# Gates and output projections of two branches with the token tiles stationary instead of the weight tiles

## The chip, the core and the metric

The kernel runs on one core of a Trainium2 chip. The metric is the device time of one execution in microseconds (us); the runs shown before are three executions, and their median is what a change is measured against. A profile is one further execution, with a record of every instruction. Engines are named as in the profile: PE is TensorE, ACT is ScalarE, DVE is VectorE, POOL is GpSimd, SP is the queue that starts most transfers.

## What is computed

One encoder block over 256 tokens of width 2048, in float32, cut here to what matters:

```python
u = rmsnorm(x)
proj = u @ w_in                 # r_q r_k r_v r_g | c_q c_kv k_pe | g_ret g_mla
ry = norm_per_head(retention(rope(r_q), rope(r_k), r_v)) * ret_norm_g
y_ret = (ry * silu(r_g)) @ w_ret_o                  # 8 heads of 256
q, k, v = lora_projections(rmsnorm(c_q), rmsnorm(c_kv), k_pe)
y_mla = attention(q, k, v) @ w_mla_o                # 16 heads of 128
merged = sigmoid(g_ret) * y_ret + sigmoid(g_mla) * y_mla
h = x + merged @ w_out
h = h + square(relu(rmsnorm(h) @ w_up)) @ w_down
return rmsnorm(h)
```

Five products of 256 x 2048 by 2048 x 2048 are touched here: the retention gate `r_g`, the gate `g_ret`, the projection `w_ret_o`, the gate `g_mla` and the projection `w_mla_o`.

## The kernel before

Every float32 product is made of three products of shorter numbers: each operand is split into a high part `hi` and a rest `lo`, and hi*hi, hi*lo and lo*hi are added up in PSUM. Activations stay in SBUF as such pairs, with features on the partitions and tokens along the row (class `Pair`: 16 feature tiles of 128, each with 256 tokens of hi and then 256 of lo). Weights come in pieces of 512 KB: `weights` (L156) loads one into `raw`, ACT rounds it to `hi` (L161), DVE takes the rest `lo` (L162). There are five `raw` buffers and four each of `hi` and `lo`, so pieces are loaded and split ahead of their use.

Two forms of product stand side by side:

- `t_unit` (L180) makes 128 output columns. A weight tile of 128 x 128 is stationary. In pass 1 (L169) the weight's hi meets both halves of an activation tile at once, a row of 512 (16 matmuls, one for each feature tile), in pass 2 (L173) the weight's lo meets the hi half, a row of 256 (16 more). The result has output features on the partitions; its two halves of 256 are added by `join` (L324: ACT copies one, DVE adds it to the other).
- `n_unit` with `n_tile` (L199 to L212) makes 512 output columns for both halves of 128 tokens. A tile of 128 tokens is stationary, and 512 columns of weights move through: for each feature tile and each half of the tokens three matmuls of 512 columns (L209 hi*hi, L210 lo*hi, L212 hi*lo), 96 in all. The result has tokens on the partitions, and nothing is to be joined.

The order of the stages on PE is: first queries and keys, `qk` (`t_unit`), values `rv` (`n_unit`), the retention gates `rg` with the retention of the eight heads between them (`ret_scores`, `ret_values`, `ret_out`), then `gr` and `yr` in turn (`gate_unit` L527, the loop at L633), the low-rank projections `cq`, `kv`, `kw`, the gates `gm` (L699), the attention in four groups of heads with its projections between, the output projection `mo`, the output product `wo` (`n_unit`, L897), and the MLP (`z`, `zs`, `dn`).

In the five stages of the change all is in `t_unit` form, 16 units each:

- `ret_gate` (L537) makes half a head's gate: join, times the inverse norms `rxb` along the row, Silu. `ret_out` (L600) transposes a head's normed retention output on PE (4 transposes of 128 x 128 into PSUM), multiplies by the gain and by the gate, and splits the product into `ry`.
- `gate` (L522) joins, multiplies by `rxb`, takes the Sigmoid; `m1` holds the `g_ret` gate, then its product with `y_ret`. `gm` holds the `g_mla` gate.
- `mla_out_begin` (L813) makes a part of the first four units of `mo` between the attention of the last heads; the loop at L860 makes the rest, and for each unit joins, multiplies by `gm`, adds `m1` and splits into the pair `mg`, which `wo` reads.

The framework schedules these stages: the instructions of each engine are put into an order when the program is built, from its own estimate of costs and from the data they depend on, so the order in the program can differ a little from that of the source. On the chip each engine takes its instructions in the order of the program. Large SBUF tiles come from a pool of six (`big`), so `hn` (the load of x for the residual, L875) takes the place of the first half of `my`, the attention's output. PSUM has four buffers for products (`mmps`) and four for transposes and attention (`atps`).

Of the kernel before, what the change touches and what calls it, by code (L numbers as in the profile page):

```python
# [19 lines left out]
P = 128  # L20
S = 256
# [77 lines left out]
def block_kernel(ctx: ExitStack, tc: tile.TileContext, A):  # L99
# [43 lines left out]
    def mmps(name):  # L143
        return pmm.tile([P, 512], F32, tag="mm", name=name)
# [179 lines left out]
    def join(out, ps):  # L324
        t = sm.tile([P, S], F32, tag="join", bufs=2, name="join")
        SC.copy(t, ps[:, S:])
        V.tensor_tensor(out=out, in0=ps[:, :S], in1=t, op=ALU.add)  # L327
# [191 lines left out]

    ry = Pair("ry")  # L520

    def gate(out, ps):  # L522
        join(out, ps)
        V.tensor_tensor(out=out, in0=out, in1=rxb, op=ALU.mult)
        SC.activation(out, out, AF.Sigmoid)

    def gate_unit(i):  # L527
        pg = mmps(f"gr{i}")
        t_unit(pg, A["w_gret"][i], x)
        gate(m1[:, i], pg)  # L530

    with tc.tile_pool(name="rp", bufs=1) as rp:
        dec = rp.tile([P, RH, 256], F32, name="dec")
        nc.sync.dma_start(dec, A["dec"])
        preps, sgs, sds, ons = {}, {}, {}, {}

        def ret_gate(u):  # L537
            h, j = divmod(u, 2)
            if j == 0:
                sgs[h] = rp.tile([P, 2, S], F32, tag="sg", bufs=2, name=f"sg{h}")  # L540
            pg = mmps(f"rg{u}")
            t_unit(pg, A["w_rg"][u], x)
            o = sgs[h][:, j]
            join(o, pg)
            V.tensor_tensor(out=o, in0=o, in1=rxb, op=ALU.mult)
            SC.activation(o, o, AF.Silu)

        def ret_prep(h):
            q, k = qk[:, 0, h], qk[:, 1, h]
            qs = rp.tile([P, 2, S], F32R, tag="qs", bufs=2, name=f"qs{h}")  # L550
            ks = rp.tile([P, 2, P], F32R, tag="ks", bufs=2, name=f"ks{h}")
            vs = rp.tile([P, 2, 2, S], F32R, tag="vs", bufs=2, name=f"vs{h}")
            split(ks[:, 0], ks[:, 1], k[:, :P])
            split(qs[:, 0], qs[:, 1], q)
            split(vs[:, 0], vs[:, 1], rv[:, :, h * S : (h + 1) * S])
            preps[h] = qs, ks, vs

        def ret_scores(h):
            q, k = qk[:, 0, h], qk[:, 1, h]
            qs, ks, _ = preps[h]  # L560
            pS = atps(f"rs{h}")
            mm3(pS[:, :S], (ks[:, 0], ks[:, 1]), (qs[:, 0], qs[:, 1]))
            PE.matmul(pS[:, S:384], k[:, P:], q[:, P:], start=True, stop=True)
            sd = rp.tile([P, 384], F32, tag="sd", bufs=2, name=f"sd{h}")
            V.tensor_tensor(out=sd[:, :S], in0=pS[:, :S], in1=dec[:, h], op=ALU.mult)
            V.tensor_tensor(out=sd[:, S:], in0=pS[:, S:384], in1=dec[:, h, :P], op=ALU.mult)
            sp = rp.tile([P, 2, 384], F32R, tag="sp", bufs=2, name=f"sp{h}")
            split(sp[:, 0], sp[:, 1], sd)
            sds[h] = sp

        def ret_values(h):
            sd = sds.pop(h)
            pO = atps(f"ro{h}")
            vs = preps.pop(h)[2]
            v0, v1 = ((vs[:, 0, t], vs[:, 1, t]) for t in range(2))
            s00, s01, s11 = ((sd[:, 0, b * P : b * P + P], sd[:, 1, b * P : b * P + P]) for b in range(3))
            mm3(pO[:, :S], s00, v0)
            mm3(pO[:, S:], s01, v0, stop=False)
            mm3(pO[:, S:], s11, v1, start=False)
            on = rp.tile([P, 2, S], F32, tag="on", bufs=2, name=f"on{h}")  # L580
            mv = rp.tile([P, 2, 2], F32, tag="mv", bufs=2, name=f"mv{h}")
            rs = rp.tile([P, 2], F32, tag="rs", bufs=2, name=f"rsd{h}")
            for t in range(2):
                st = rp.tile([P, 6], F32, tag="st", bufs=2, name=f"st{h}{t}")
                V.bn_stats(st, pO[:, t * S : (t + 1) * S])
                V.bn_aggr(mv[:, t], st)
            V.tensor_scalar(rs, mv[:, :, 1], EPS, None, op0=ALU.add)
            G.tensor_tensor(out=rs, in0=rs, in1=negh, op=ALU.pow)
            for t in range(2):
                V.tensor_scalar(  # L590
                    on[:, t],
                    pO[:, t * S : (t + 1) * S],
                    mv[:, t, 0:1],
                    rs[:, t : t + 1],
                    op0=ALU.subtract,
                    op1=ALU.mult,
                )
            ons[h] = on

        def ret_out(h):  # L600
            on, sg = ons.pop(h), sgs.pop(h)
            pT = atps(f"rt{h}")
            for j in range(2):
                for t in range(2):
                    o = j * S + t * P
                    PE.transpose(pT[:, o : o + P], on[:, t, j * P : (j + 1) * P], ident)
            for j in range(2):
                e = 2 * h + j
                V.scalar_tensor_tensor(
                    sg[:, j],  # L610
                    in0=pT[:, j * S : (j + 1) * S],
                    scalar=vec[:, V_RET + e : V_RET + e + 1],
                    in1=sg[:, j],
                    op0=ALU.mult,
                    op1=ALU.mult,
                )
            split(*ry.span(2 * h, 2), sg)

        ret_prep(0)
        for h in range(RH):  # L620
            ret_gate(2 * h)
            ret_scores(h)
            if h + 1 < RH:
                ret_prep(h + 1)
            if h:
                ret_out(h - 1)
            ret_gate(2 * h + 1)
            ret_values(h)
        m1 = big("m1")
        gate_unit(0)  # L630
        ret_out(RH - 1)

    for i in range(KT):  # L633
        if i:
            gate_unit(i)
        py = mmps(f"yr{i}")
        t_unit(py, A["w_ret_o"][i], ry)
        V.tensor_tensor(out=m1[:, i], in0=joined(py), in1=m1[:, i], op=ALU.mult)

    with ExitStack() as mctx:  # L640
        cc = big("cc", F32R, shape=(P, 2 * LT, 2, S))
# [53 lines left out]
                SC.activation(kn[:, t, j], pkv[t][1][:, 224:288], AF.Copy, scale=rx[:, t : t + 1])  # L695
        cn = lora_norm(1, [(t, 288 * j, pkv[t][j][:, : 288 - 64 * j]) for j in range(2) for t in range(2)])

        gm = big("gm")
        for i in range(KT):  # L699
            pg = mmps(f"gm{i}")  # L700
            t_unit(pg, A["w_gmla"][i], x)
            gate(gm[:, i], pg)
            if i == 0:
                lora_turn(1, cn)
                pk = atps("pk")
                for t in range(2):
                    PE.transpose(pk[:, t * P : (t + 1) * P], kn[:, t].rearrange("p j n -> p (j n)"), ident)
                rope(kpe, pk[:, :S], *tabs[1], 32)
                lp.close()
                mp = mctx.enter_context(tc.tile_pool(name="mp", bufs=1))  # L710

        my = Pair("my")
        heads, probs, outs = {}, {}, {}
# [61 lines left out]
        def mla_projections(g):  # L775
# [34 lines left out]
            SC.copy(v1, pss[1])  # L810
            heads[g, "v"] = vs, v1

        def mla_out_begin():  # L813
            for i in range(4):
                mo[i] = mmps(f"mo{i}")
                w = weights(A["w_mla_o"][i][:, :HK], [P, HK, P])
                for k in range(0, HK, 4):
                    wk = w[0][:, k : k + 4], w[1][:, k : k + 4]
                    t_pass1(mo[i], wk, my, k, 4, k == 0)
                    t_pass2(mo[i], wk, my, k, 4, False)  # L820
                    yield
            for i in range(4):
                w = weights(A["w_mla_o"][i][:, HK : HK + 4], [P, 4, P])
                t_pass1(mo[i], w, my, HK, 4, False)
                t_pass2(mo[i], w, my, HK, 4, False)
                yield

            for i in range(4):
                w = weights(A["w_mla_o"][i][:, 12:], [P, 4, P])
                mo[i] = mo[i], w  # L830
                t_pass1(mo[i][0], (w[0][:, :2], w[1][:, :2]), my, 12, 2, False)
                t_pass2(mo[i][0], (w[0][:, :2], w[1][:, :2]), my, 12, 2, False)
                yield

        SLOTS = (
            ((0, 2, 4, 6), (4, 6, 8, 10), (6, 8, 10, 12)),
# [20 lines left out]
        for g in range(4):  # L857
            interleave(mla_projections(g), mla_attention(g - 1) if g else iter(()))
        interleave(mla_out_begin(), mla_attention(3))
        for i in range(KT):  # L860
            if i in mo:
                pm, w = mo[i]
                t_pass1(pm, (w[0][:, 2:], w[1][:, 2:]), my, 14, 2, False)
                t_pass2(pm, (w[0][:, 2:], w[1][:, 2:]), my, 14, 2, True)
            else:
                pm = mmps(f"mo{i}")
                t_unit(pm, A["w_mla_o"][i], my)
            t = joined(pm)
            V.tensor_tensor(out=t, in0=t, in1=gm[:, i], op=ALU.mult)
            V.tensor_tensor(out=t, in0=t, in1=m1[:, i], op=ALU.add)  # L870
            split(mg.hi(i), mg.lo(i), t)

    rctx.close()
    hn = big("hn", shape=(P, 2, D))
# [334 lines left out]
```

## Time and profile before

| | |
|---|---|
| median of three runs | 1618.09 us (1618.04 to 1618.14) |
| the profiled execution | 1618.44 us, of which 1616.7 us from its first to its last instruction |
| granted TensorE clock | 0.998 of full speed |
| PE busy | 1601.8 us, 99% of the span |
| DVE busy | 1089.9 us, 67% |
| ACT busy | 889.2 us, 55% |
| POOL busy | 67.4 us, 4% |
| transfers | 325.41 MB, 201 GB/s on average |

The share of busy time is an average over stages. Matmuls are pipelined, so their recorded durations overlap: what one costs is read from the distance between two starts, not from its duration. Times below are counted from the first instruction of the span. Stages by their first matmul: `rv` 101.64, `rg` 188.71, `gr` and `yr` 293.50, `cq` 472.95, `gm` 520.66, the attention 610.80, `mo` 723.86, `wo` 825.18, `z` 914.94 us.

### The profile page before, as it was taken

What the parts mean: (1) busy time and instruction counts of PE and PEld (TensorE: products, weight loads), DVE (VectorE), ACT (ScalarE), POOL (GpSimd) and SP (SyncE); (2) the same over time, 40 slices, a digit from 0 to 9 for tenths busy, and PEclk for the clock granted to TensorE, in tenths of its full rate; (3) what the DMA queues carried; (4) which work ended last, traced back from release to release, by engine and by line L of the source; (5) the groups of instructions that cost most, each with busy time, mean ns of one, the idle gap of its engine ahead of it and who ended that gap; (6) DMA issues with size and microseconds to landing.
All of it is one profiled execution on the core that took longest, in us unless ns stands there. A gap on an engine that the chain in (4) does not pass through costs nothing.

```text
span 1616.7 us, 22933 instructions
## 1 busy us (share of the span) xinstructions
PE 1601.8 (99%) x8566; PEld 1380.2 (85%) x8566; DVE 1089.9 (67%) x1568; ACT 889.2 (55%) x1393; POOL 67.4 (4%) x94
## 2 busy tenths in 40 slices
PE   8999999999999999999999999999999999999997
PEld 6888888888889889888888888888888888888886
DVE  7974588655555657775767689887978555555555
ACT  6544555544445546665545576676766544444444
POOL 7100000000000000000000000000000000000001
PEclk9999999999999999999999999999999999999999
DMA  8665544555556554334574677666676766666663
GB/s 309 201 230 195 184 157 161 176 186 194 192 172 194 195 185 144 131 111 146 199 243 173 225 241 241 215 229 217 215 282 237 238 219 214 219 219 217 218 211 114
DMA packets 94815, 325.41 MB, mean 201 GB/s; under 512 B 10736, under 2 KB 15984, under 8 KB 93680
## 3 DMA queue, kind: packets, MB, share of 16 engines
q1 hardware_dynamic: 92000, 313.46, 57.7%
q0 software_dynamic: 2560, 8.39, 1.8%
q10 hardware_dynamic: 144, 2.10, 0.4%
q8 instruction: 67, 1.10, 0.3%
q14 instruction: 44, 0.36, 0.1%
HBM read 311.33 MB, written 12.58 MB: 200 GB/s over the span
## 4 chain that ended last, share of the span: by engine, by line
PE 97%; DVE 1%; DMA 0%; issue 0%; ACT 0%; POOL 0%; SPq 0%; DVEq 0%; POOLq 0%; ACTq 0%
PE z L169 9%; PE dn L1067 7%; PE dn L1066 7%; PE dn L1068 7%; PE z L173 5%; PE rg L169 4%; PE yr L169 4%; PE gr L169 4%; PE gm L169 4%; PE mo L169 4%; PE zs L295 2%; PE zs L296 2%; PE zs L297 2%; PE qk L169 2%; PE gr L173 2%; PE yr L173 2%
## 5 line engine op out<-in xcount | busy, mean ns | idle before, releaser
L162 DVE TENSOR_TENSOR lo<-raw,hi 128x1024 fp32r<-128x1024 f32 (+2 forms) x434 | 514.5, 1200 | 366.2 <-ACT hi L161 238.2
L161 ACT CAST hi<-raw 128x1024 fp32r<-128x1024 f32 (+2 forms) x434 | 446.0, 1029 | 389.5 <-PE dn L1068 96.6
L1068 PE MATMUL dn<-hi,dl 128*128 128x512 f32 x512 | 199.3, 389 | 0.0
L1067 PE MATMUL dn<-lo,dh 128*128 128x512 f32 x512 | 199.3, 389 | 0.0
L1066 PE MATMUL dn<-hi,dh 128*128 128x512 f32 x512 | 197.7, 389 | 0.0
L169 PE MATMUL z<-hT,hi 128*128 128x512 f32 x640 | 159.5, 391 | 0.0
L169 PEld LDWEIGHTS z<-hT,hi 128*128 128x128 f32 x640 | 117.4, 188 | 22.6
L1066 PEld LDWEIGHTS dn<-hi,dh 128*128 128x128 f32 x512 | 96.0, 188 | 20.0
L1068 PEld LDWEIGHTS dn<-hi,dl 128*128 128x128 f32 x512 | 96.1, 188 | 19.9
L1067 PEld LDWEIGHTS dn<-lo,dh 128*128 128x128 f32 x512 | 96.1, 188 | 19.8
L337 DVE TENSOR_TENSOR lo<-raw,hi 128x1024 fp32r<-128x1024 f32 x80 | 94.9, 1222 | 19.1 <-ACT hi L336 18.9
L173 PEld LDWEIGHTS z<-hT,lo 128*128 128x128 f32 x640 | 87.3, 190 | 6.2
L173 PE MATMUL z<-hT,lo 128*128 128x256 f32 x640 | 89.2, 282 | 0.0
L336 ACT CAST hi<-raw 128x1024 fp32r<-128x1024 f32 x80 | 80.4, 1049 | 7.4 <-PE wo L210 5.0
L336 ACT CAST dh<-hl 128x256 fp32r<-128x256 f32 x64 | 26.0, 407 | 90.9 <-PE dn L1067 86.9
L169 PE MATMUL mo<-my,hi 128*128 128x512 f32 x256 | 65.5, 396 | 0.4 <-DVE val L327 0.4
L336 ACT CAST shi<-forms 128x1024 fp32r<-128x1024 f32 x48 | 50.5, 1053 | 25.4 <-DVE forms L266 17.7
L169 PE MATMUL rg<-x,hi 128*128 128x512 f32 x256 | 64.0, 395 | 0.0
L337 DVE TENSOR_TENSOR slo<-forms,shi 128x1024 fp32r<-128x1024 f32 x48 | 58.2, 1221 | 4.9 <-ACT shi L336 4.9
L169 PE MATMUL yr<-ry,hi 128*128 128x512 f32 x256 | 61.4, 391 | 0.0
L169 PE MATMUL gr<-x,hi 128*128 128x512 f32 x256 | 61.3, 391 | 0.0
L169 PE MATMUL gm<-x,hi 128*128 128x512 f32 x256 | 61.1, 391 | 0.0
(324 smaller groups left out, 2949.7 us busy)
## 6 DMA issues: line engine op xcount, KB each, us to landing
raw<-w_down SPq DMA_DIRECT2D x128, 512.0 KB, 4.4
raw<-w_up SPq DMA_DIRECT2D x80, 512.0 KB, 4.5
raw<-w_rv SPq DMA_DIRECT2D x32, 512.0 KB, 4.7
raw<-w_rg SPq DMA_DIRECT2D x32, 512.0 KB, 4.4
raw<-w_gret SPq DMA_DIRECT2D x32, 512.0 KB, 4.3
raw<-w_ret_o SPq DMA_DIRECT2D x32, 512.0 KB, 4.4
raw<-w_gmla SPq DMA_DIRECT2D x32, 512.0 KB, 4.5
raw<-w_out SPq DMA_DIRECT2D x32, 512.0 KB, 4.3
```

The source lines that it names most:

```text
L161: SC.copy(hi, raw)
L162: V.tensor_tensor(out=lo, in0=raw, in1=hi.bitcast(F32), op=ALU.subtract)
L169: PE.matmul(out, w[0][:, k], x.both(k0 + k), start=start and k == 0, stop=False)
L173: PE.matmul(out[:, :S], w[1][:, k], x.hi(k0 + k), start=False, stop=stop and k == n - 1)
L295: PE.matmul(q, ah, hi[:, o], start=first, stop=False)
L296: PE.matmul(q, al, hi[:, o], start=False, stop=False)
L297: PE.matmul(q, ah, lo[:, o], start=False, stop=last)
L336: SC.copy(hi, val)
L337: V.tensor_tensor(out=lo, in0=val, in1=hi.bitcast(F32), op=ALU.subtract)
L1066: mm(PE.matmul(out, dh[:, ts], hi[:, ws], start=i == 0, stop=False))
L1067: mm(PE.matmul(out, dh[:, ts], lo[:, ws], start=False, stop=False))
L1068: mm(PE.matmul(out, dl[:, ts], hi[:, ws], start=False, stop=end))
```

## The change

All five products go from `t_unit` to `n_unit` form: tokens are stationary and 512 columns of weights move, four blocks of 512 columns for each product. The weights are laid out for it on the host (`_n_units` in place of `_t_units`). The gates are then made by one activation for each 128 tokens and 512 columns straight from PSUM, with the inverse norm of each token as its scale, so the joins and the products with `rxb` go. `m1` and `gm` hold tokens on the partitions. The retention gates are one generator that is drawn on two steps at a time, each a piece of 12 matmuls; a head's gate is multiplied in before the transposes, and `ret_out` runs two heads behind instead of one. `mla_out_begin` makes the first three quarters of two blocks of `mo` in twelve steps. `merge` multiplies and adds with tokens on the partitions, and `merge_turn` transposes 4 feature tiles (8 transposes of 128 x 128) and splits them into `mg`, since `wo` needs features on the partitions.

```diff
-    def gate(out, ps):
-        join(out, ps)
-        V.tensor_tensor(out=out, in0=out, in1=rxb, op=ALU.mult)
-        SC.activation(out, out, AF.Sigmoid)
-
-    def gate_unit(i):
-        pg = mmps(f"gr{i}")
-        t_unit(pg, A["w_gret"][i], x)
-        gate(m1[:, i], pg)
+    def n_cols(name, src, x, c, between=()):
+        pss = [mmps(f"{name}{c}{t}") for t in range(2)]
+        todo = iter(between)
+        for kq in range(4):
+            n_unit(pss, src[4 * c + kq], x, 4 * kq, 4, kq == 0, kq == 3)
+            fn = next(todo, None)
+            if fn:
+                fn()
+        return pss
+
+    def gate_cols(name, src, out, c, between=()):
+        pss = n_cols(name, src, x, c, between)
+        for t in range(2):
+            SC.activation(out[:, t, c * 512 : (c + 1) * 512], pss[t], AF.Sigmoid, scale=rx[:, t : t + 1])
...
+        def ret_gates():
+            for g in range(RH // 2):
+                pss = [mmps(f"rg{g}{t}") for t in range(2)]
+                for kq in range(4):
+                    for kh in range(2):
+                        src = A["w_rg"][4 * g + kq][:, 2 * kh : 2 * kh + 2]
+                        n_unit(pss, src, x, 4 * kq + 2 * kh, 2, kq == kh == 0, (kq, kh) == (3, 1))
+                        if (kq, kh) != (3, 1):
+                            yield
+                sgs[g] = rp.tile([P, 2, 512], F32, tag="sg", bufs=2, name=f"sg{g}")
+                for t in range(2):
+                    SC.activation(sgs[g][:, t], pss[t], AF.Silu, scale=rx[:, t : t + 1])
+                yield
...
         def ret_out(h):
-            on, sg = ons.pop(h), sgs.pop(h)
+            on = ons.pop(h)
+            sg = sgs[h // 2][:, :, h % 2 * S : h % 2 * S + S]
+            V.tensor_tensor(out=on, in0=on, in1=sg, op=ALU.mult)
...
         for h in range(RH):
-            ret_gate(2 * h)
+            next(gates)
+            next(gates)
             ret_scores(h)
...
-            if h:
-                ret_out(h - 1)
-            ret_gate(2 * h + 1)
+            if h > 1:
+                ret_out(h - 2)
+            next(gates)
+            next(gates)
             ret_values(h)
...
+        m1 = big("m1", shape=(P, 2, D))
+        gate_cols("gr", A["w_gret"], m1, 0, [lambda: ret_out(RH - 2), lambda: ret_out(RH - 1)])
+
+    for c in range(4):
+        if c:
+            gate_cols("gr", A["w_gret"], m1, c)
+        cs = slice(c * 512, (c + 1) * 512)
+        for t, ps in enumerate(n_cols("yr", A["w_ret_o"], ry, c)):
+            V.tensor_tensor(out=m1[:, t, cs], in0=ps, in1=m1[:, t, cs], op=ALU.mult)
...
+        for c in range(4):
+            gate_cols("gm", A["w_gmla"], gm, c, [None, late_turn] if c == 0 else ())
...
+        def mo_part(c, kp):
+            src = A["w_mla_o"][4 * c + kp // 2][:, kp % 2 * 2 : kp % 2 * 2 + 2]
+            n_unit(mo[c], src, my, 2 * kp, 2, kp == 0, kp == 7)
+
         def mla_out_begin():
...
+            for c in range(2):
+                mo[c] = [mmps(f"mo{c}{t}") for t in range(2)]
+            for kps in (range(4), range(4, 6)):
+                for c in range(2):
+                    for kp in kps:
+                        mo_part(c, kp)
+                        yield
...
+        def merge(c):
+            cs = slice(c * 512, (c + 1) * 512)
+            for t, ps in enumerate(mo[c]):
+                V.tensor_tensor(out=gm[:, t, cs], in0=ps, in1=gm[:, t, cs], op=ALU.mult)
+                V.tensor_tensor(out=gm[:, t, cs], in0=gm[:, t, cs], in1=m1[:, t, cs], op=ALU.add)
+
+        def merge_turn(c):
+            for jj in range(2):
+                pT = atps(f"mt{c}{jj}")
+                for j in range(2):
+                    for t in range(2):
+                        o = j * S + t * P
+                        k = 4 * c + 2 * jj + j
+                        PE.transpose(pT[:, o : o + P], gm[:, t, k * P : (k + 1) * P], ident)
+                split(*mg.span(4 * c + 2 * jj, 2), pT.rearrange("p (j n) -> p j n", j=2))
+
+        for c in range(2):
+            for kp in (6, 7):
+                mo_part(c, kp)
+            merge(c)
+        for c in range(2, 4):
+            mo[c] = n_cols("mo", A["w_mla_o"], my, c, [None, lambda: merge_turn(c - 2), lambda: merge_turn(c - 1)][: c])
+            merge(c)
+        for c in (2, 3):
+            merge_turn(c)
```

Read closely, `merge_turn` is called five times: for block 0 inside block 2 of `mo`, for blocks 1 and 2 inside block 3, and after the loop for block 2 once more and for block 3.

More of the change, by code (lines that the diff above doesn't have):

```diff
@@ L535, in block_kernel @@
         preps, sgs, sds, ons = {}, {}, {}, {}
[L537 to L546, printed above, removed]
+        def ret_gates():
[11 more added lines that the diff above has]
+                yield
         def ret_prep(h):
@@ L579, in ret_values @@
             mm3(pO[:, S:], s11, v1, start=False)
-            on = rp.tile([P, 2, S], F32, tag="on", bufs=2, name=f"on{h}")
+            on = rp.tile([P, 2, S], F32, tag="on", bufs=3, name=f"on{h}")
             mv = rp.tile([P, 2, 2], F32, tag="mv", bufs=2, name=f"mv{h}")
@@ L608, in ret_out @@
                 e = 2 * h + j
[L609 to L617, printed above, removed]
+                split(ry.hi(e), ry.lo(e), pT[:, j * S : (j + 1) * S], scale=vec[:, V_RET + e : V_RET + e + 1])
         ret_prep(0)
+        gates = ret_gates()
         for h in range(RH):
-            ret_gate(2 * h)
+            next(gates)
+            next(gates)
             ret_scores(h)
@@ L624, in block_kernel @@
                 ret_prep(h + 1)
-            if h:
-                ret_out(h - 1)
-            ret_gate(2 * h + 1)
+            if h > 1:
+                ret_out(h - 2)
+            next(gates)
+            next(gates)
             ret_values(h)
[L629 to L638, printed above, removed]
+        m1 = big("m1", shape=(P, 2, D))
[6 more added lines that the diff above has]
+            V.tensor_tensor(out=m1[:, t, cs], in0=ps, in1=m1[:, t, cs], op=ALU.mult)
     with ExitStack() as mctx:
@@ L696, in block_kernel, with late_turn @@
         cn = lora_norm(1, [(t, 288 * j, pkv[t][j][:, : 288 - 64 * j]) for j in range(2) for t in range(2)])
[L698 to L710, printed above, removed]
+        gm = big("gm", shape=(P, 2, D))
+        def late_turn():
+            lora_turn(1, cn)
+            pk = atps("pk")
+            for t in range(2):
+                PE.transpose(pk[:, t * P : (t + 1) * P], kn[:, t].rearrange("p j n -> p (j n)"), ident)
+            rope(kpe, pk[:, :S], *tabs[1], 32)
+        for c in range(4):
+            gate_cols("gm", A["w_gmla"], gm, c, [None, late_turn] if c == 0 else ())
+        lp.close()
+        mp = mctx.enter_context(tc.tile_pool(name="mp", bufs=1))
         my = Pair("my")
@@ L811, in mla_projections @@
             heads[g, "v"] = vs, v1
+        def mo_part(c, kp):
+            src = A["w_mla_o"][4 * c + kp // 2][:, kp % 2 * 2 : kp % 2 * 2 + 2]
+            n_unit(mo[c], src, my, 2 * kp, 2, kp == 0, kp == 7)
         def mla_out_begin():
[L814 to L833, printed above, removed]
+            for c in range(2):
[5 more added lines that the diff above has]
+                        yield
         SLOTS = (
@@ L859, in block_kernel @@
         interleave(mla_out_begin(), mla_attention(3))
[L860 to L871, printed above, removed]
+        def merge(c):
[7 more added lines that the diff above has]
+                for j in range(2):
+                    for t in range(2):
+                        o = j * S + t * P
[11 more added lines that the diff above has]
+            merge_turn(c)
     rctx.close()
@@ L1179 @@
         "w_rv": _n_units(s_rv),
-        "w_rg": _t_units(s_rg),
-        "w_gret": _t_units(s_gret),
-        "w_ret_o": _t_units(np.asarray(w_ret_o)[0]),
+        "w_rg": _n_units(s_rg),
+        "w_gret": _n_units(s_gret),
+        "w_ret_o": _n_units(np.asarray(w_ret_o)[0]),
         "w_cq": np.ascontiguousarray(s_cq.reshape(8, 2, P, 512).transpose(0, 2, 1, 3)),
@@ L1186 @@
         ),
-        "w_gmla": _t_units(s_gmla),
+        "w_gmla": _n_units(s_gmla),
         "w_qpe": four(qb[:, :, 128:]),
@@ L1191 @@
         "w_v": _n_units(np.ascontiguousarray(kvb[:, :, 128:]).reshape(LORA, D)),
-        "w_mla_o": _t_units(np.asarray(w_mla_o)[0]),
+        "w_mla_o": _n_units(np.asarray(w_mla_o)[0]),
         "w_out": _n_units(np.asarray(w_out)[0]),
```

## The prediction

> **What bounds the kernel now.** I read the page's first part and its chain of waits first.
>
> ```profile
> PE 1601.8 (99%) x8566; PEld 1380.2 (85%) x8566; DVE 1089.9 (67%) x1568; ACT 889.2 (55%) x1393; POOL 67.4 (4%) x94
> PE 97%; DVE 1%; DMA 0%; issue 0%; ACT 0%; POOL 0%; SPq 0%; DVEq 0%; POOLq 0%; ACTq 0%
> ```
>
> The chain that ended last is PE for 97%; every other engine has a third of its time or more to spare. So the question is how much PE time each form of product takes, and whether PE has to wait anywhere new. Next, the sums over stretches of time, taken for the stages `rv` (all in the new form), `gr` with `yr` (all in the old form) and `wo` (new form with transposes in it).
>
> ```profile
> core 0: us, PE busy (x) PEld busy (x) DVE busy (x) ACT busy (x) POOL busy (x), PEclk, DMA share, GB/s
> 101.64:188.71 87.07, 87.07 (x386) 72.08 (x385) 43.95 (x44) 39.90 (x46) 0.00 (x0) 1.00 0.62 206
> 293.50:472.95 179.45, 179.45 (x1037) 158.61 (x1036) 103.48 (x140) 86.39 (x115) 0.69 (x1) 1.00 0.56 188
> 825.18:914.94 89.76, 89.76 (x411) 74.58 (x409) 57.53 (x68) 43.78 (x60) 0.00 (x0) 1.00 0.62 217
> ```
>
> The second number of each row is the length of the stretch, the next PE's busy time in it: they are equal, and the granted clock is 1.00. PE never stands still in these stages, in either form. Last the order of time on PE, in three places: the steady `gr`/`yr` loop, the first transposes in `wo`, and the end of the begun units of `mo`.
>
> ```profile
> 311.52 3.82 PE L169 MATMUL yr<-ry,hi 128*128 128x512 f32 x16
> 315.17 2.08 PE L173 MATMUL yr<-ry,lo 128*128 128x256 f32 x16
> 317.08 3.82 PE L169 MATMUL gr<-x,hi 128*128 128x512 f32 x16
> ...
> 852.42 1.03 PE L885 MATMUL ht<-con,hn 128*128 128x128 f32 x8
> 853.21 0.48 PE L209 MATMUL wo<-hi,mg 128*128 128x512 f32 x1
> 853.53 0.40 PE L210 MATMUL wo<-hi,mg 128*128 128x512 f32 x1
> ...
> 757.45 0.40 PE L173 MATMUL mo<-my,lo 128*128 128x256 f32 x2
> 758.26 2.11 PE L169 MATMUL mo<-my,hi 128*128 128x512 f32 x8 [0.41 <-DVE val L327]
> ```
>
> The first column is the start. One old unit takes 317.08 - 311.52 = 5.56 us: 3.65 for 16 rows of 512 (228 ns each) and 1.91 for 16 rows of 256 (119 ns each).
>
> **The sum, part by part.**
>
> *Matmuls.* An old unit is 128 output columns. In the chain's own list pass 1 of `yr` starts at 311.68 and again, 28 units of `gr` and `yr` later, at 467.55 us: 5.567 us each. The `rv` stage is four blocks of 512 columns in 87.07 us, 21.77 each, so 5.442 us for 128 columns. The number of streamed columns is the same in both (16 x 768 against 24 x 512 = 12,288); what differs is the number of matmuls, 32 against 24: two rows of 256 take 239 ns and one of 512 takes 227, so every matmul has about 12 ns that don't depend on its length, and eight of them are gone. Five products of 16 units are 80 units, and each is 5.567 - 5.442 = 0.125 us shorter: **-10.0 us**. All of it is on the path, as PE was busy without a gap in these stages. `wo` confirms the block: 89.76 us less three sets of transposes (below) is 87.1, four blocks of 21.8.
>
> The Trainium skill (TensorE: Matmul & The Clock Gate, Back-to-back issue gap) speaks against this size: it gives an isolated gap of N / 2.4 + 2.5 ns, a fixed part of only 2.5 ns for each matmul. By that, eight matmuls fewer are 20 ns a unit, and 80 units 1.6 us instead of 10.0. This trace disagrees: its fixed part is 12 ns, and the two unit times above hold it whole.
>
> *Transposes.* The merged branches now have tokens on the partitions, and each turn puts 8 transposes on PE. Eight of the same kind (`ht`, float32, 128 x 128) and the matmul after them run from 852.42 to 853.53, 1.11 us; less that matmul's 0.227 it is 0.88 us for a set. There are five sets, not four: block 2 is turned twice. 5 x 0.88 = **+4.4 us**, on the path, since PE is in order and has no gap to hide them in. The transposes of `ret_out` and of the low-rank parts are as many as before and only move.
>
> *A wait that goes.* At 757.45 two rows of 256 start, the second at about 757.56, and the next matmul at 758.26: 0.70 us after it where 0.12 is the rule. It waits for DVE to free a PSUM buffer (the fifth unit of `mo` needs the first one's). In the new order 21 matmuls (4.8 us) or more lie between a begun block's last one and the first that needs its buffer, against 0.69 us for the product that frees it (row of `hn<-wo,hn`, 128x512 from PSUM, 688 ns). **-0.6 us**. Nothing else is late there.
>
> *ACT and DVE.* The 80 joins go (ACT 374 ns, DVE 419 each) and the 48 products with `rxb` (420); 48 gate activations of 128x256 (410) become 24 of 128x512 (687 by `rv`'s eviction); the remaining products are half as many and twice as long (426 to 688). `ret_out` gains a DVE product of 128x512 for each head (about 0.69 us), and the split of `mg` comes from PSUM (10 of ACT 0.6 and DVE 0.69, by `my`'s split). DVE and ACT both lose more than they gain, and neither is on the path: **0**. What hides them is the ring of split weights: in `wo` DVE waits for ACT and ACT for PE, so about three pieces of 2.72 us are ready ahead. If that cover went, each block's end would show.
>
> *Queues.* SP starts four transfers fewer (eight of 256 KB become four of 512). The load of `hn` (2 MB, 8.7 us to landing) stands behind six pieces of `w_out` instead of seven and waits for PE's last read of the first half of `my`. That read was in the last unit of `mo`, some 2 us before `wo`; now it is in the second quarter of the last block, 10.9 us before. The weights queued behind it start sooner, not later: **0**. POOL has the same instructions.
>
> *The seam between `mo` and `wo`.* Block 3's turn needs its four DVE steps of 0.69 us, with one weight rest (1.23) and one split (0.69) between them in DVE's order: from about 1.1 us before the last matmul of `mo` has gone to 3.6 after. On PE the repeated turn of block 2 (0.88) and 19 matmuls of `wo` (4.3) stand before the first transposes of block 3, which come at 5.2. So it costs **0**, with 1.6 us to spare. Without that cover the loss is at most 3.6 us; a gain is excluded, since nothing waited there. I take 0, for the `wo` stage shows the same pattern (`ht` behind the DVE sum of the block before) without a gap. `wo` itself needs block 3 only 16 us in.
>
> *The retention stage.* Its 104.8 us are filled too (PE busy throughout). The gates are drawn in steps of 2 x 2.72 = 5.44 us where a unit took 5.57, so the scores' way over DVE and ACT has 0.13 us less cover a step, but also four DVE steps fewer in it. I take 0; if a wait came back in each of the eight heads it would be the 0.13 us difference, 1 us together. The longer filling between the last heads' attention (twelve pieces of 2.72 us in place of sixteen of 1.39) can only cover more.
>
> Sum: -10.0 + 4.4 - 0.6 = -6.2 us. From the profiled 1618.44 (1616.7 and 1.7 around it) that is 1612.2; the profiled run is 0.35 above the median of 1618.09, so the forecast is **1611.9 us**, 0.38% less. A measurement of this kernel can tell about 0.2% (3.2 us) from no change: 1614.9 is the edge.
>
> **Rivals.**
>
> *Only streamed columns count.* If PE's time went with the columns alone, the first term would be nothing, and the change adds 4.4 us of transposes: 1618.1 + 4.4 - 0.6 = 1621.9 us, slower by 0.24%. For it: the columns are exactly equal, and weight loads (PEld 85%) look like a second limit that doesn't care. Against it: rows of 256 start 119 ns apart with weight loads of 188 ns each, so loads overlap, and the two unit times differ over whole stages. The change loses at all from a fixed part under 6 ns a matmul on (80 x 8 x 6 = 3.8 us, what the other terms add). Chance 4%. With the 2.5 ns of the Trainium skill (the same page and section) the time would be 1618.1 - 1.6 + 4.4 - 0.6 = 1620.3 us, and the trace speaks against that as above.
>
> *Block ends hold the weights up.* DVE's products now wait for a block's last matmul, with weight rests queued behind them and PE waiting for those. To undo the gain it must cost PE 6.2 us over 20 blocks, 0.3 us at each: 1618 us, or slower with more. For it: DVE has 9.8 us of rests, 2.8 of merging and 2.8 of splits in a block of 21.8 us of `mo`. Against it: that is 70%, the wait is under one matmul group, three pieces lie ahead, and `wo`, with the same products at its block ends, has no gap. Chance 6%.
>
> *The seam's cover fails, or the retention stage waits.* Some 2 to 3.6 us are lost at one or both: 1614 to 1615.5 us. The order on PE and DVE speaks against it, but 1.6 us of slack is not much. Chance 10%.
>
> **The numbers.** The forecast, 1610.8 to 1613.5 us, has 80%; its spread is 1 us of the retention stage above and about 1 us below, if the small excess of `rg` and `mo` over their units (0.5 and 1 us) goes too. The third rival is taken in up to 1615.2, which leaves out some 12%. Faster by over 0.2%: the forecast and six of the third rival's ten, 86%. Within 0.2%: the rest of it and half of the second rival, 7%. Slower: the first rival and the other half, 7%.
>
> **What would show it.** Right: the old stages shrink in the sums over stretches, `gr` with `yr` from 179.45 to about 175.0, and `gm` (to the start of the attention at 610.80) from 90.1 to 88.1, each with its transposes; 40 transposes of 128 x 128 named `mt<-con,gm`, 109 ns apart; no wait above 0.3 us on PE between 188 and 910 us; DVE's busy time down by some 55 us without effect. Wrong: a distance other than 227 ns between the new matmuls, a gap on PE ahead of block 3's transposes, or waits for `hi` or `lo` at block ends.

## The result, and the profile after

The changed kernel took **1613.97 us** (median of ten runs, 1612.44 to 1615.59), the kernel before beside it on the same chip 1618.24 (1617.68 to 1618.65): a ratio of **0.9974, 95% interval 0.9965 to 0.9984**. That is 4.3 us less, where 6.2 were forecast. The time lies 2.1 us above the forecast itself and 0.5 above the range of 1610.8 to 1613.5 us that had 80%; it falls into the part up to 1615.2 that was taken in for the third rival. The profiled execution of the changed kernel took 1614.23 us, 1612.4 of it from the first to the last instruction, at a granted clock of 0.997.

The first part of the page after, and its chain of waits:

```profile
PE 1597.1 (99%) x7966; PEld 1351.1 (84%) x7966; DVE 1045.3 (65%) x1406; ACT 861.6 (53%) x1287; POOL 69.1 (4%) x94
PE 97%; DVE 1%; DMA 1%; ACT 0%; issue 0%; POOL 0%; SPq 0%; DVEq 0%; POOLq 0%; ACTq 0%
```

PE is the bound as before, with 600 matmuls fewer (8566 to 7966: 640 gone from the five products, 40 transposes new). DVE and ACT lost 44.6 and 27.6 us of work, and neither was on the path. Only one share of the chain is new: DMA has 1% where it had 0.

The sums over four stretches of the changed kernel: `rv` (untouched), `gr` with `yr`, `gm`, and `wo`. The second number is the stretch's length, the next PE's busy time in it.

```profile
101.27:188.33 87.06, 87.06 (x386) 72.08 (x385) 43.93 (x44) 39.89 (x46) 0.00 (x0) 1.00 0.62 207
290.95:466.88 175.93, 175.93 (x785) 145.76 (x784) 87.63 (x84) 75.88 (x79) 0.69 (x1) 1.00 0.59 191
514.57:602.76 88.19, 88.19 (x396) 73.08 (x395) 46.03 (x51) 41.65 (x53) 0.69 (x1) 1.00 0.60 201
818.16:908.93 90.77, 90.77 (x419) 75.44 (x418) 59.11 (x69) 45.13 (x63) 0.00 (x0) 1.00 0.57 197
```

PE fills every stretch, in the new form as in the old. `gr` with `yr` went from 179.45 to 175.93 and `gm` from 90.14 to 88.19; `wo` has one us more, as transposes now lie in it. The whole difference by stages, each from its first matmul to the next stage's:

| stage | before | after | difference |
|---|---|---|---|
| ahead of `rv` (`qk` and the warm-up) | 101.64 | 101.27 | -0.38 |
| `rg` | 104.79 | 102.61 | -2.18 |
| `gr`, `yr` | 179.45 | 175.93 | -3.52 |
| `gm` | 90.14 | 88.19 | -1.95 |
| `mo` | 101.32 | 102.36 | +1.04 |
| `wo` | 89.75 | 90.77 | +1.02 |
| **the changed stages** | | | **-5.59** |
| `rv`, `cq` to `gm`, attention, `z` | 265.46 | 265.42 | -0.04 |
| `zs`, the up-projection of the MLP | 319.23 | 320.83 | **+1.60** |
| `dn` to the end | 364.89 | 365.05 | +0.16 |

The first row is no gain: in the ten profiles of this document the time ahead of `rv` lies between 100.72 and 102.01 us, whatever the kernel.

So the changed stages gained 5.6 us, close to the 6.2 of the forecast, and 1.6 us were lost again between 28 and 74 us after the end of the changed stages, in a stage whose code is the same. The order of time on PE shows where: two waits that the profile before has not.

```profile
937.46 0.72 PE L169 MATMUL z<-hT,hi 128*128 128x512 f32 x2 [0.37 <-ACT hs L964]
982.38 0.50 PE L297 MATMUL zs<-slo,hc 128*128 128x512 f32 x1 [0.60 <-DVE slo L337]
```

The square brackets hold the idle time ahead of the instruction and what ended it. They make 0.97 of the 1.60 us: each counts from the recorded end of the matmul ahead, 0.39 us after its start, where without a wait the next one starts after 0.23, so a wait costs more than its bracket. The rest `slo` came late from DVE, and DVE itself had stood still a few steps earlier (order of time on DVE, after):

```profile
973.51 1.22 DVE L337 TENSOR_TENSOR lo<-raw,hi 128x1024 fp32r<-128x1024 f32 x1
976.37 1.23 DVE L266 TENSOR_TENSOR forms<-raw,sraw 128x1024 f32<-128x1024 f32 x1 [1.63 <-DMA raw<-w_up_s]
```

It waited 1.63 us for one load of up weights (`w_up_s`, 512 KB). The same instruction in the profile before waited 0.21 us:

```profile
980.28 1.23 DVE L266 TENSOR_TENSOR forms<-raw,sraw 128x1024 f32<-128x1024 f32 x1 [0.21 <-DMA raw<-w_up_s]
```

From the start of that load's issue to DVE's start were 3.59 us before and 5.01 after. The experiments had two questions: is the 5.6 us made of the terms that the forecast gave it, and does the loss in `zs` belong to the change?

### The profile page after: what moved, and what is told of

Same layout as the page of the kernel before. It is cut to its first block, busy times and chain, and to the rows that moved or that the text cites. A ratio compares the mean times of both kernels' runs of the same rounds, so it can differ in the third digit from the quotient of the medians.

```text
span 1612.4 us, 21370 instructions
## 1 busy us (share of the span) xinstructions
PE 1597.1 (99%) x7966; PEld 1351.1 (84%) x7966; DVE 1045.3 (65%) x1406; ACT 861.6 (53%) x1287; POOL 69.1 (4%) x94
## 3 DMA queue, kind: packets, MB, share of 16 engines
q8 instruction: 62, 1.02, 0.2%
## 4 chain that ended last, share of the span: by engine, by line
PE 97%; DVE 1%; DMA 1%; ACT 0%; issue 0%; POOL 0%; SPq 0%; DVEq 0%; POOLq 0%; ACTq 0%
PE z L169 9%; PE dn L1074 7%; PE dn L1076 7%; PE dn L1075 7%; PE z L173 5%; PE zs L297 2%; PE zs L295 2%; PE zs L296 2%; PE qk L169 2%; PE mo L209 2%; PE rg L210 2%; PE rg L209 2%; PE rg L212 2%; PE mo L210 2%; PE mo L212 2%; PE gr L210 2%
## 5 line engine op out<-in xcount | busy, mean ns | idle before, releaser
L162 DVE TENSOR_TENSOR lo<-raw,hi 128x1024 fp32r<-128x1024 f32 (+1 forms) x430 | 519.4, 1210 | 411.0 <-ACT hi L161 408.2
L161 ACT CAST hi<-raw 128x1024 fp32r<-128x1024 f32 (+1 forms) x430 | 445.8, 1038 | 455.0 <-PE dn L1076 96.5
L1082 POOL DMA_DIRECT2D hl<-hid x32 | 17.7, 554 | 1019.4 <-DVE dl L337 550.8
L964 ACT COPY hs<-z 128x512 f32<-128x512 f32 x40 | 23.4, 586 | 64.8 <-PE z L173 62.7
L337 DVE TENSOR_TENSOR dl<-hl,dh 128x256 fp32r<-128x256 f32 x64 | 27.1, 425 | 38.5 <-ACT dh L336 38.5
L209 PE MATMUL mo<-hi,my 128*128 128x512 f32 x128 | 51.0, 401 | 0.0
L209 PE MATMUL rg<-hi,x 128*128 128x512 f32 x128 | 50.7, 396 | 0.0
```

Source lines behind the costliest of these rows:

```text
L161: SC.copy(hi, raw)
L162: V.tensor_tensor(out=lo, in0=raw, in1=hi.bitcast(F32), op=ALU.subtract)
L209: PE.matmul(out, x.hi(k0 + k, ts), w[0][:, k], start=start and k == 0, stop=False)
L337: V.tensor_tensor(out=lo, in0=val, in1=hi.bitcast(F32), op=ALU.subtract)
```

## The experiments

Each ratio is to runs of the kernel before on the same chip. A stage's length comes from each run's own profile, by its first matmuls.

**The changed kernel again**, nothing edited.

> The changed kernel once more. The profile after shows the five changed stages with wo 5.6 us shorter (6.2 were forecast), and the untouched MLP stage (zs, from its first matmul to that of dn) 1.6 us longer, in two places where PE waits for ACT and DVE, which wait for a transfer. If the second is chance (theory A: transfers land later in some executions, and ACT stands in order behind the first reload of hid), this profile has the changed stages within 0.2 us of the first and zs at another length, anywhere from 319.2 to 321. If it comes with the change (theory B: other SBUF places or an order that differs), zs is 320.8 us again with the same two gaps of about 0.6 to 0.9 us.

Measured: 1613.19 us, ratio 0.9966 (0.9954 to 0.9979). All five changed stages had the lengths of the first profile to 0.01 us. `zs` took 320.21. The wait at its start was gone and that at 55 us was there again, with 0.68 us. So the changed stages repeat exactly; of the two waits in `zs` the first came in one execution alone (ACT stood 3.23 us for a transfer back from DRAM, `dh<-hl`, with `hs<-z` queued behind it; here it stood 2.36 and nothing was late), the second came again.

**One turn of block 2 instead of two.**

```diff
-        for c in (2, 3):
-            merge_turn(c)
+        merge_turn(3)
```

> The changed kernel with the second turn of block 2 left out (four turns instead of five). Theory A: eight transposes fewer, 0.88 us less between mo and wo, so some 0.9 us under the repeat, if the MLP stage is alike. A rival: the repeated turn covered the wait of block 3's turn for its DVE steps, so PE then waits at the seam and most of the 0.88 us stays; the transposes come 4.3 us after the last matmul of mo, and the DVE steps need some 3 us without the repeated split, so I expect no gap.

Measured: 1612.79 us, 0.9966 (0.9953 to 0.9978). `mo` went from 102.36 to 101.56 and `wo` from 90.77 to 90.67: 0.90 us for one set of eight transposes, where the forecast counted 0.88. PE had no gap at the seam from `mo` to `wo`. The program now puts 23 matmuls of `wo` in front of block 3's transposes where there were 19 and the set, so they come 5.2 us after the last of `mo` again, and not at the 4.3 that was expected; DVE's last step for them was done after 3.0 us. Only 0.4 us of the 0.9 show in the median, and `zs` took 320.63 with a wait of 0.77 us at 55 us.

**Rows of 256 in `gm` alone.** Each matmul of 512 columns becomes two of 256 with the same weights, but for the first and the last of each sum.

```diff
+        cols = [slice(c, c + 256) for c in (0, 256)] if short[0] else [slice(None)]
...
-            PE.matmul(out, x.lo(k0 + k, ts), w[0][:, k], start=False, stop=False)
+            for cs in cols:
+                PE.matmul(out[:, cs], x.lo(k0 + k, ts), w[0][:, k, cs], start=False, stop=False)
```

> The changed kernel with the gate product gm cut into rows of 256 columns where it had 512 (all but the first and the last matmul of a group), 368 matmuls more with the same columns. If each matmul costs a fixed 12 ns, the gm stage is 368 x 12.4 = 4.6 us longer (2 x 119.6 - 226.8 = 12.4). If PE's time goes with columns alone it is unchanged. With a fixed part of 2.5 ns, the figure of the Trainium skill, it is 0.9 us longer.

Measured: 1618.16 us, 1.0000 (0.9991 to 1.0009): the gain of the whole change is gone. The stretch of `gm`:

```profile
514.45:607.50 93.05, 93.05 (x765) 92.36 (x764) 46.03 (x51) 41.73 (x53) 0.69 (x1) 1.00 0.56 191
```

It streams the columns of the 88.19 us above and has 368 matmuls more (the row shows 369: a few records can be missing); it takes 4.86 us longer, **13.2 ns for each**. That is close to the 12.4 ns of the forecast, measured with nothing else changed, and it rules out the rival that only columns count. By the 2.5 ns that the Trainium skill gives for an isolated gap (TensorE: Matmul & The Clock Gate, Back-to-back issue gap) it would have been 0.9 us, by estimate.

Is this a fixed part of every matmul, as the forecast took it? The third pair of the row says that the weight loads are busy for 92.36 of 93.05 us, 99%, against 83% of the stretch with rows of 512. The Trainium skill says in the same section that in a stream of weight loads and matmuls the spacing is set by both. The busy share alone does not settle it here: a load is recorded with 188 ns in both stretches, more than the 120 ns between two rows of 256, so the records overlap.

A third row length in the same profiles speaks against 12 ns for every matmul. In the profile before, 48 matmuls of 288 columns (`kv` and `kw`, 494.74 to 500.98 us) follow each other without a gap, 130.1 ns apart; 12.4 ns and the columns would make it 133.0. A straight line through 288 and 512 columns leaves some 6 ns at no columns and puts a row of 256 at 116.3 ns, where 119.6 are measured. So by this estimate, which takes the time as linear between the two lengths, about half of the 12 or 13 ns is a fixed part, and the other half is extra in rows as short as 256. Where that half comes from, the loads or something else, no run here shows. For this change, which trades two rows of 256 for one of 512, it comes to the same.

**The retention gates alone in the new form**; the four other products are as before.

```diff
-            ret_gate(2 * h)
+            next(gates)
+            next(gates)
...
+        gate_unit(0)
+        ret_out(RH - 2)
+        ret_out(RH - 1)
```

> The kernel before with the retention gates alone in the new form (ret_gates and ret_out as in the change, the other four products as before). 16 units x 0.125 = 2.0 us less in the stages rg, gr and yr together, no transposes added: 0.9988 of before. If the gain came from elsewhere (the joins, or the wait at mo), it is under 0.5 us. In the profile after, rg is 102.6 us (104.8 before, of which 0.44 by a set of transposes that moved on).

Measured: 1616.29 us, 0.9989 (0.9980 to 0.9998). `rg` took 102.61, as in the whole change, so its -2.18 are its own. But `gr` with `yr` took 179.93, 0.48 more than before: `ret_out` of one more head now falls into it. Together they are -1.70 us, where 16 units of 0.125 are 2.0. Taken with the same 0.48, the -3.52 of `gr` and `yr` in the whole change are -4.00, to the digit the 32 units of 0.125. So the 0.3 us that lack lie in the retention stage. PE has no gap there; the starts around the small transposes and short matmuls of the heads are further apart (from a matmul of 128 columns of the scores to the next start 101 ns on average where it was 71, from a transpose 89 where it was 68). Why was not settled.

**PE's program moved on a little.** What delays one load in a stage with the same code? In the profiles, queue 8 (kind "instruction", 62 packets of 16 KB in the page after, one in some 26 us) had a packet under way just when the slow load should have landed. The count of these packets goes with PE's program: in each of the ten profiles there are 256 to 258 recorded matmuls and weight loads for one packet (17,132 for 67 before, 15,932 for 62 after). The theory was that PE's own instructions are fetched over the same DMA engines, that the fetch collides with the load, and that fewer matmuls ahead of it moved the fetch there. If so, small matmuls put where PE waits anyway, on its warm-up before the first data, must move it away or bring it in. The edit went into the version with one turn (36 matmuls) and into the kernel before (30):

```diff
+    for _ in range(36):
+        PE.matmul(spin[:, :32], cold[:, :P], cold[:, :32], start=True, stop=True)
```

> The four-turn version with 36 small matmuls (128x32) more at the start, right after the warm-up matmuls; nothing else differs, in no engine's order. Three executions with the change had a gap of 0.6 to 0.8 us on PE 55 us into zs: DVE waits there for a load of w_up_s, and a transfer of the instruction queue q8 (16 KB, about 1 us, one each 24 us) starts 46 to 47.5 us into zs, while that load is under way; before and the version with the retention gates alone have the q8 transfer at 52 and 53 us and no gap, the gm256 version has it at 47.5 and no gap. Theory C: q8 brings PE's instructions, and the change moved these transfers onto that load. Then 72 instructions more bring them some 7 us earlier (about 40 us into zs), and the gap goes: zs 319.2 to 319.8 instead of 320.6. Rival (theory B): it comes with the changed SBUF places or order, and zs stays at 320.2 to 320.8 with the gap. A difference of the start-up time (before rv) belongs to the added matmuls and is left out.

Measured: **1611.72 us, 0.9960 (0.9946 to 0.9974)**, the shortest median of all, 1.07 us under that of the same kernel without the edit. `zs` took 319.23 us, as in the profile before, with no gap; the fetch started 38.3 us into the stage instead of 47.1.

> The kernel before with 30 such small matmuls more at the start. Theory C: the q8 transfer at 52.3 us into zs comes to about 46.5, onto the load of w_up_s, and zs is 0.6 to 0.8 us longer than the 319.2 of before, with a gap at 55 us. Rival: zs stays at 319.2 to 319.6, and the loss belongs to the change or is chance.

Measured: 1618.40 us, 1.0004 (0.9995 to 1.0013). The old kernel, with none of the change in it, now has the wait too. From the order of time on PE:

```profile
986.86 0.50 PE L297 MATMUL zs<-slo,hc 128*128 128x512 f32 x1 [0.67 <-DVE slo L337]
```

Its fetch had moved from 52.3 to 47.1 us into the stage, the load took 5.08 us instead of 3.59, and `zs` grew by 0.96 us to 320.19. The median is only 0.4 us above that of the kernel before beside it, inside the noise; the profile shows the wait.

**The reloads of the MLP put in order.** With the first three `dh` and `dl` splits kept behind the up-projection in the order of the program, ACT should not stand in front of `hs<-z` while a reload is under way (the first of the two waits). Made on the version with one turn:

```diff
-        split(dh, dl, hl[:, i % 2])
+        pin = tc.keep_in_program_order if n < 3 else (lambda ins: ins)
+        pin(SC.copy(dh, hl[:, i % 2]))
+        pin(V.tensor_tensor(out=dl, in0=hl[:, i % 2], in1=dh.bitcast(F32), op=ALU.subtract))
```

> The four-turn version with the first splits of the hidden layer for w_down (dh on ACT, dl on DVE) kept behind the MLP's work instead of early in zs, where ACT stands 2.3 to 3.2 us behind the reload of hid. If that wait costs PE time by itself (a gap of 0.4 us at 11 us into zs in one of the executions), such gaps go, and zs loses the 0.1 to 0.5 us of it; the gap at 55 us, which waits for another transfer, stays. The seam to dn may lose up to 1 us, as the splits then come late. I expect a total within 0.7 us of the four-turn version.

Measured: 1619.00 us, 1.0004 (0.9995 to 1.0013), 6.2 us above the version with one turn where at most 0.7 was expected: a miss. From the order of time on PE:

```profile
1257.23 0.50 PE L1073 MATMUL dn<-hi,dh 128*128 128x512 f32 x1 [3.91 <-ACT dh L1085]
```

The splits that had been ready long before now come after the last activation of the up-projection, and the first matmul of `dn` waits 3.91 us for them. `zs` and `dn` together took 691.1 us, 5.4 more than with one turn alone. A rare wait of 0.4 us had been traded for a steady one of ten times that.

**The changed kernel itself, with PE's program moved on** by the same 36 small matmuls and nothing else.

> The changed kernel with nothing taken out, and 36 small matmuls (32 columns) on PE's warm-up, before any of its data has come, where PE waits anyway. They only move the later instructions on in PE's program, and with them the places where PE's next instructions are fetched. Theory (the loss in the up-projection of the MLP is an instruction fetch that meets one load of up weights): the changed stages keep their lengths to 0.05 us (rg 102.6, gr and yr 175.9, gm 88.2, mo 102.4, wo 90.8), the fetch leaves the 44 to 50 us of that stage, the load is back at about 3.6 us, the gap of 0.6 us at 55 us is gone, and the stage zs takes 319.2 to 319.8 us instead of 320.2 to 320.8; the median is 1612.4 to 1612.9, some 0.9 us above the version without the second turn of block 2. Rival (the loss belongs to the change itself, through the state of the rings of weights when the MLP begins): the gap stays at 55 us, zs 320.2 or more, and the median 1613.2 to 1614.

Measured: **1612.37 us, 0.9959 (0.9946 to 0.9973)**. This was on another chip, with 1618.78 us for the kernel before beside it. The changed stages have their lengths to the digit, `zs` took 319.23 us, and no wait is in it. The same DVE instruction as above:

```profile
975.04 1.23 DVE L266 TENSOR_TENSOR forms<-raw,sraw 128x1024 f32<-128x1024 f32 x1 [0.25 <-DMA raw<-w_up_s]
```

The transfers between the issue of that load and this start, in the changed kernel (971.35 to 976.37 us) and then with the shift (971.41 to 975.04). Columns are packets, MB, and share of 16 engines' time:

```profile
q1 hardware_dynamic: 402, 1.09, 74.1%
q8 instruction: 1, 0.02, 1.1%
```

```profile
q1 hardware_dynamic: 316, 0.77, 65.7%
```

The fetch is in the first and not in the second. It is small, 1.1% of 16 engines' time in 5.02 us, which is 0.88 us of one engine; yet the load took 5.01 us beside it and 3.63 without. Why 0.88 us become 1.4 was not settled.

All ten profiles together:

| kernel | fetch starts, us into `zs` | load to DVE, us | wait at 55 us |
|---|---|---|---|
| before | 52.3 | 3.59 | none |
| retention gates alone | 53.4 | 3.62 | none |
| one turn, moved on | 38.3 | 3.49 | none |
| changed, moved on | 37.9 | 3.63 | none |
| rows of 256 in `gm` | 47.5 | 3.85 | none |
| changed | 47.5 | 5.01 | 0.60 |
| changed, again | 45.7 | 5.09 | 0.68 |
| one turn | 47.1 | 5.18 | 0.77 |
| reloads put in order | 46.8 | 4.96 | 0.54 |
| before, moved on | 47.1 | 5.08 | 0.67 |

Wherever a fetch starts 45 to 48 us into the stage the load is late, with one exception: with rows of 256 the fetch began 3.2 us after the load's issue, in the five late ones 1.5 to 3.0 us after it, so that the load had nearly landed. That this is why it escaped is likely and not shown. That the fetch is the cause rests on the three shifts, each profiled once: they add nothing to the data's transfers, and the wait went, came and went with them.

It is not a rule for every load. Over the other loads of up and down weights in the ten profiles, 89 met a fetch 1.5 to 3.0 us after their issue; 30 of these landed more than 0.5 us later than the median of the same load in the profiles where it met none, and 9 more than 1 us. Of 1,849 loads that met none, 90 and 20 were as late.

## Why the prediction was right, point by point

The way and the terms of the changed stages were right: they gave -5.6 us for -6.2. The whole came out at -4.3, and its time stands in the part of the range that the third rival was given. But the seam had no loss at all and the retention stage one of 0.3 us, so it was not that rival that brought it there; it was for the most part the step on the queues, the last point below. In so far it is luck that the time still lies inside.

- **Matmuls, -10.0 us: right.** `gr` with `yr` is 4.00 us shorter without the moved `ret_out`, `gm` 1.95 where 2.0 was counted. Rows of 256 cost 13.2 ns each. That this is a fixed part of every matmul, the forecast's reason, is by the rows of 288 true of about half of it; the sum does not need it, as it goes by the two unit times. Of its signs, the 175.0 us for `gr` with `yr` was too low: 32 units take 4.0 off 179.45, which leaves 175.45, and the moved transposes add 0.48; the 175.93 measured is just that. The rival that only columns count (1621.9 us) is dead. The new matmuls start 227 ns apart, as the forecast said (order of time on PE, in `gm`):

```profile
519.78 0.39 PE L212 MATMUL gm<-lo,x 128*128 128x512 f32 x1
520.01 0.39 PE L209 MATMUL gm<-hi,x 128*128 128x512 f32 x1
520.23 0.39 PE L210 MATMUL gm<-hi,x 128*128 128x512 f32 x1
520.46 0.39 PE L209 MATMUL gm<-hi,x 128*128 128x512 f32 x1
```

- **Transposes, +4.4 us: right.** 0.90 us for a set against 0.88, by taking one away. The group of transposes is there with 40, and in the order of time on PE at the seam a set of eight takes 0.79 us to the first `wo` matmul after it, which is some 0.09 longer than the others to its next start; no wait is ahead:

```profile
816.91 0.62 PE L212 MATMUL mo<-lo,my 128*128 128x512 f32 x2
817.37 1.03 PE L868 MATMUL mt<-con,gm 128*128 128x128 f32 x8
818.16 0.48 PE L209 MATMUL wo<-hi,mg 128*128 128x512 f32 x1
...
822.57 0.38 PE L868 MATMUL mt<-con,gm 128*128 128x128 f32 x2
822.71 0.48 PE L210 MATMUL wo<-hi,mg 128*128 128x512 f32 x1
...
825.32 0.82 PE L868 MATMUL mt<-con,gm 128*128 128x128 f32 x6
```

- **The wait that goes, -0.6 us: right.** The 0.41 us of idle time at the end of the begun units of `mo` is not in the profile after; it is still there with the retention gates alone. `mo` and `wo` together are +2.06 us where these three terms make +1.8 (-2.0, +4.4, -0.6); five sets of 0.90 explain 0.1 of the 0.26.
- **The seam, 0: right.** The first of block 3's transposes come at 822.57 us, 5.20 us after the start of the repeated turn, which follows `mo`'s last matmul (817.37): the 5.2 of the forecast. What they wait for, the last DVE step of block 3, was done 1.6 us before, at 820.96, which is the 1.6 us to spare of the forecast (order of time on DVE):

```profile
820.28 0.68 DVE L859 TENSOR_TENSOR gm<-gm,m 128x512 f32<-128x512 f32 x1
```

Six of the eight come later still, at 825.32.
- **The retention stage, 0 (up to 1 us): mis-sized by 0.3 us**, inside the margin that the forecast gave it. No wait returned; the time is in the starts between the heads' small matmuls.
- **ACT and DVE, 0: right**, though the size given for DVE was not: 44.6 us less instead of some 55. The removed and added instructions sum to -57.9 by their recorded durations, but these overlap where instructions follow at once (a 128x256 step is recorded with 0.42 us and the next starts 0.34 us later).
- **Queues, 0: the step that failed.** It followed the data's transfers and found them no later, which is right; it did not count that PE's instructions are loaded too, and that a change in their number moves these loads against the data's. The stages up to `wo` have no wait from that, but `zs` lost 1.0 us in the repeat (320.21, against 319.23 with the fetch elsewhere) and 1.6 in the profiled execution, in which the 0.37 us wait for the reload came on top.

The sum of the terms was -6.2 us; the changed stages gave -5.6, and `zs` took back 1.0 to 1.6. The -4.3 measured lie between the two sums that this gives. With the fetch out of the way the median is 1612.37, 6.4 us under the kernel before beside it. That is nearer to the -6.2 than the -5.6 of the stages warrants, so part of the match is scatter of the medians. The rival that weights are held up at block ends did not come: no wait for `hi` or `lo` is found on PE in the changed stages.

## What to carry to other kernels

Where PE is filled, count rows by their length, not only columns: two equal float32 products differed because two rows of 256 take 239 ns and one of 512 takes 227, and that can be read from the distance of two starts in the old profile. Read a gain by stages, and look at untouched stages too: 1.0 to 1.6 of 5.6 us were lost here after the last changed stage. When an untouched stage moves, compare the landing times of its loads between profiles before the change is blamed; shifting the program by a few idle instructions tells a coincidence from a consequence.

## What the runs showed of the hardware

By these traces PE's program is loaded while it runs, in 16 KB packets, one for 256 to 258 matmuls and weight loads, of 0.9 to 2.6 us each and 20 to 29 us apart around `zs`; the profile counts them on the same 16 DMA engines as the weights. Five times a packet that began 1.5 to 3.0 us after the issue of one 512 KB load went with a delay of some 1.4 us (from the issue to DVE's start 5.0 to 5.2 us for 3.5 to 3.6), and in a stage with little lead PE then stood for 0.5 to 0.8 us and the stage grew by 1.0 to 1.4. Other loads that met a packet in that way were late by more than 0.5 us in 30 of 89 cases. Where the packets fall depends on the number of PE's instructions ahead: 36 small matmuls moved one from 47.5 to 37.9 us into the stage.
